# A two-block network on one core: in the feed-forward parts, gate and up are computed with tokens on partitions and turned, down moves both parts of its operand at once, and GpSimd's work there goes to ScalarE and VectorE

## The chip, the core and the metric

The kernel runs on one core of a Trainium2 chip. The metric is the device time of one execution in microseconds (us): the median of the kernel before is 1747.96 us over three runs (1747.33 to 1749.26). The engines are TensorE (PE; its weight loads are PEld), VectorE (DVE), ScalarE (ACT), GpSimd (POOL) and SyncE (SP), whose queue issues nearly all transfers.

## The reference

The input is 256 tokens of 1024 features in fp32. A first block of two layers is followed by a second block of one layer; the second block also reads 256 tokens of a context, and its modulation vectors come from two vectors `c` and `c_ctx`. Cut to what the change touches:

```
def swiglu_ffn(x, norm, w_gate, w_up, w_down):        # D_MODEL 1024, D_FF 2816
    h = rms_norm(x, norm)
    return (silu(h @ w_gate) * (h @ w_up)) @ w_down

for l in range(2):                                     # first block
    x = x + 0.5 * swiglu_ffn(x, ffn1_norm[l], ...)
    x = x + mixer(x)                                   # attention, chunk attention, retention
    x = x + 0.5 * swiglu_ffn(x, ffn2_norm[l], ...)

mx = silu(c) @ w_ada + b_ada                           # second block: six vectors of 1024
mc = silu(c_ctx) @ w_ada + b_ada                       # the same for the context (two are used)
x = x + gm_x * rms_norm(mixer2(modulate(rms_norm(x), ...), context))
x = x + gf_x * rms_norm(swiglu(modulate(rms_norm(x), ...), w_gate, w_up, w_down))
```

So there are five feed-forward parts: `ffn1` and `ffn2` in each of two layers, and one in the second block.

## The kernel before

Products keep nearly fp32 precision: every operand is split into a high part (`hi`, rounded to the short format fp32r) and a low part (`lo`, what is left), and `mm3` (L200) makes each product from three matmuls: low by high, high by low, high by high. Weights arrive in chunks of 1 MB (`load_now`, L170 to 192): SP issues the transfer into one of three `raw` buffers, ScalarE casts the high part (L189) and VectorE subtracts for the low part (L190), 1024 elements at a time, into four buffers each of `hi` and `lo`, which hold two chunks.

Activations lie with features on partitions: `x` is eight tiles of 128 features by 256 tokens, and `Stream` (L346) makes their two parts, `xh` and `xl`, as x comes.

`swiglu` (L363) runs gate and up in 22 steps of 128 hidden features. In a step the weights are the stationary operand and the tokens move: 2 x 8 x 3 = 48 matmuls of 256 columns. The two results share a PSUM bank. `gated` then multiplies them by 1/rms of each token (VectorE, L377), takes tanh (ScalarE), forms the product (VectorE L382, then GpSimd L384 in the first block, VectorE in the second), casts the high part `hh` (ScalarE, L386) and subtracts the low part `hl` (VectorE, L387). The result has hidden features on partitions, which is what the down product needs: 8 steps of 22 x 3 = 66 matmuls of 256 columns, with the weights stationary again. PSUM has a pool of four banks `mm` for these products and one of four banks `sm` for small ones.

Beside three of these parts (`ffn1` of layer 0, `ffn2` of layer 0, `ffn1` of layer 1) the modulation vectors are made (`ada`, L864): for each 128 features, 512 KB of weights `adaw` are multiplied by the silu of `c` and summed along the row. `swiglu` calls `tick` once a step, which asks for one more such piece. Where the piece is needed for two vectors, or is one of every second of the others, GpSimd multiplies and ScalarE sums (L886, L887); else VectorE does both in one instruction (L889). Beside `ffn2` of layer 1 the context is computed in the same way. The sums of squares for the norms are made by `Squares` (L222): seven squares and all additions on GpSimd, one square on ScalarE.

TensorE's order is that of the code. The order of the other engines is made by a scheduler that works with estimated times and priorities; loads are raised by 10 places (`AHEAD`).

Of the kernel before, what the change touches and what calls it, by code (L numbers as in the profile page):

```python
# [36 lines left out]
# columns of the per-feature table  # L37
# [12 lines left out]
# columns of a layer's row table, and of the second block's  # L50
# [10 lines left out]
def constants():  # L61
    """Tables that depend on shapes alone."""
# [42 lines left out]
def tile_kernel(ctx, tc, a):  # L105
# [35 lines left out]
    for half in range(2):  # L141
        xt = new(xp, [P, 4, T], "x", bufs=2)
        nc.sync.dma_start(xt.rearrange("p k t -> p (k t)"), a["xT"][half])
        x += [xt[:, k, :] for k in range(4)]
        if half == 0:
            first = new(wp, [P, RAW], "raw")
            for p in range(2):
                nc.sync.dma_start(first[:, half_sub(p)], a["wgu_ffn1"][0, 0, :, half_sub(p)])
    for p in range(2, 4):
        nc.sync.dma_start(first[:, half_sub(p)], a["wgu_ffn1"][0, 0, :, half_sub(p)])  # L150
# [14 lines left out]
    def load(src, n, eng=V):  # L165
        """A chunk of weights, and its two parts of 12 bits each."""
# [39 lines left out]
    def warm(n, bank=psm):  # L206
        """Products that nothing reads: they keep the tensor engine's clock up while it waits."""
# [6 lines left out]
    def rstd(ss, n, scale, eps, tag):  # L214
        """(ss * scale + eps) ** -0.5 over a few columns."""
# [6 lines left out]
    class Squares:  # L222
        """The sum of squares of each token, added up as the features come."""
# [4 lines left out]
        def add(self, t):  # L228
            self.n += 1
            if self.n == KD:  # L230
                q = new(tp, [P, T], "sqt", bufs=4)
                S.activation(q, t, AF.Square)
                if self.urgent:
                    self.parts = [self.acc, q]
                else:
                    G.tensor_tensor(self.acc, self.acc, q, op=ALU.add)
                    self.parts = [self.acc]
            elif self.acc is None:
                self.acc = new(tp, [P, T], "sqa", bufs=2)
                G.tensor_tensor(self.acc, t, t, op=ALU.mult)  # L240
            else:
                q = new(tp, [P, T], "sqt", bufs=4)
                G.tensor_tensor(q, t, t, op=ALU.mult)  # L243
                G.tensor_tensor(self.acc, self.acc, q, op=ALU.add)

        def by_token(self):
            """1/rms with tokens on partitions."""
# [15 lines left out]
        def along_row(self, keep=True):  # L263
            """The same along the free axis, on all partitions."""
# [11 lines left out]
    class QuickSquares(Squares):  # L276
        """The same of what comes in PSUM, with little left to do after the last part."""
# [29 lines left out]
    class DenseSquares(Squares):  # L307
        """The same, added up by the tensor engine, which it keeps busy between the parts."""
# [22 lines left out]
        def by_token(self):  # L331
            self.flush()
            # all rows are the same: the diagonal has each token on its partition
# [12 lines left out]
    class Stream:  # L346
        """What the next part of the first block needs of x, made as x comes."""
# [15 lines left out]
    def swiglu(xh, xl, sq, wgu, wd, fp, done, tick=lambda: None):  # L363
        """done(m, psum): each 128 output features of twice (four times with sq) the block's product."""
        hh, hl = [], []
        first_ks = [[k] for k in range(KD)] if sq is None else [range(KD - 2), range(KD - 2, KD)]
        # by then the sums of squares are there
        ready = 1 if first else 0

        def gated(gt, up, ps):  # L370
            if sq is not None:
                gu_t = new(fp, [P, 2, T], "gu", bufs=2)
                if ps is None:
                    for i, p in enumerate((gt, up)):
                        V.tensor_tensor(gu_t[:, i, :], p, sq.rb, op=ALU.mult)
                else:
                    V.tensor_tensor(gu_t, ps, bc_mid(sq.rb, 2), op=ALU.mult)  # L377
                gt, up = gu_t[:, 0, :], gu_t[:, 1, :]
            th = new(fp, [P, T], "th", bufs=2)
            S.activation(th, gt, AF.Tanh, scale=0.5)  # L380
            t1 = new(fp, [P, T], "t1", bufs=2)
            V.scalar_tensor_tensor(t1, th, 1.0, gt, op0=ALU.add, op1=ALU.mult)  # L382
            h = new(fp, [P, T], "h", bufs=2)
            (G if sq is not None else V).tensor_tensor(h, t1, up, op=ALU.mult)  # L384
            a_, b_ = new(fp, [P, T], "hh", F32R, bufs=KF), new(fp, [P, T], "hl", F32R, bufs=KF)
            S.copy(a_, h)  # L386
            V.tensor_tensor(b_, h, raw(a_), op=ALU.subtract)  # L387
            hh.append(a_)
            hl.append(b_)

        waiting = []
        for j in range(KF):
            w = load(wgu[j], 2 * D)
            if j or ready:
                ps = psm([P, 2, T])
                pss = [ps[:, gu, :] for gu in range(2)]
            else:
                # the last parts of x come late: the first product begins with the others
                ps = None
                pss = [psm([P, T]) for _ in range(2)]  # L400
# [1194 lines left out]
```

## Time and profile before

| | |
|---|---|
| device time, three runs | 1747.33, 1747.96, 1749.26 us |
| span of the profiled execution | 1745.7 us |
| median of the runs less this span | 2.3 us |
| TensorE matmul, busy | 1680.7 us (96%), 12837 instructions |
| TensorE weight load, busy | 1613.0 us (92%) |
| VectorE, busy | 1310.7 us (75%) |
| ScalarE, busy | 916.4 us (52%) |
| GpSimd, busy | 547.3 us (31%) |
| mean granted TensorE clock | 0.989 |
| transfers | 317.54 MB, mean 182 GB/s |

The profiled execution has no time of its own beside the span; the 2.3 us is what the median of the runs adds to it. A matmul's recorded duration is longer than the distance to the next one, since matmuls are pipelined; the cost of one in a row of many is the distance from start to start. In the profile's stretches, the number behind an engine's busy time is the count of its instructions there.

### The profile page before, as it was taken

The page shows a single profiled execution, that of the slowest core. Times are in us where ns is not written, and L with a number is a line of the kernel's source. Part 1 is how long each engine was busy: PE and PEld are TensorE (multiplying, and loading weights), DVE is VectorE, ACT ScalarE, POOL GpSimd, SP SyncE. Part 2 cuts the span into 40 slices and gives each one's busy share as a digit, 9 for nine tenths or more (in the row PEclk, how much of TensorE's full clock was granted, in tenths as well). Part 3 has the DMA queues.
Part 4 walks back from the last instruction along what each step waited for, and adds up shares of the span by engine and source line. Part 5 has one row for each costly group of instructions (what it writes and reads, how often), then busy time and mean ns, then how long its engine had stood idle before and what let it go on. Part 6 is the DMA issues. An engine that isn't in the chain of part 4 may idle for free. (4 is left out here: it accounts for less than half of the span.)

```text
span 1745.7 us, 31442 instructions
## 1 busy us (share of the span) xinstructions
PE 1680.7 (96%) x12837; PEld 1613.0 (92%) x12837; DVE 1310.7 (75%) x1755; ACT 916.4 (52%) x1491; POOL 547.3 (31%) x521
## 2 busy tenths in 40 slices
PE   8899999999999999999999999999999997999998
PEld 8789978899989999999987899999999996789997
DVE  8986678666899766986678766777887699766654
ACT  5554456634455544554456644455665564454443
POOL 5741242001466223651242101261333255410002
PEclk9999999999999999999999999999999998999999
DMA  8554664345477557764664435475445443035543
GB/s 315 196 197 155 207 225 166 124 145 190 170 260 267 183 167 266 282 242 162 193 246 145 167 124 172 156 259 196 165 144 171 142 150 129 26 132 182 186 155 119
DMA packets 55584, 317.54 MB, mean 182 GB/s; under 512 B 6160, under 2 KB 8592, under 8 KB 28816
## 3 DMA queue, kind: packets, MB, share of 16 engines
q1 hardware_dynamic: 51408, 307.45, 50.9%
q10 hardware_dynamic: 4032, 8.09, 1.3%
q8 instruction: 100, 1.64, 0.4%
q14 instruction: 44, 0.36, 0.1%
HBM read 314.46 MB, written 1.05 MB: 181 GB/s over the span
## 5 line engine op out<-in xcount | busy, mean ns | idle before, releaser
L190 DVE TENSOR_TENSOR lo<-raw,hi 128x1024 fp32r<-128x1024 f32 (+2 forms) x580 | 716.2, 1247 | 208.5 <-ACT hi L189 206.9
L189 ACT CAST hi<-raw 128x1024 fp32r<-128x1024 f32 (+2 forms) x584 | 562.9, 968 | 449.3 <-PE mm L204 360.9
L202 PE MATMUL mm<-xh,lo 128*128 128x256 f32 x2272 | 650.5, 286 | 29.8 <-DVE lo L190 29.8
L203 PE MATMUL mm<-xl,hi 128*128 128x256 f32 x2272 | 645.8, 284 | 0.1
L204 PE MATMUL mm<-xh,hi 128*128 128x256 f32 x2272 | 645.2, 284 | 0.0
L202 PEld LDWEIGHTS mm<-xh,lo 128*128 128x128 f32 x2272 | 438.4, 193 | 36.2 <-DVE lo L190 34.8
L203 PEld LDWEIGHTS mm<-xl,hi 128*128 128x128 f32 x2272 | 438.4, 193 | 0.6 <-DVE xl L953 0.3
L204 PEld LDWEIGHTS mm<-xh,hi 128*128 128x128 f32 x2272 | 438.4, 193 | 0.0
L202 PE MATMUL mm<-hh,lo 128*128 128x256 f32 x880 | 246.9, 281 | 0.0
L203 PE MATMUL mm<-hl,hi 128*128 128x256 f32 x880 | 246.6, 280 | 0.0
L204 PE MATMUL mm<-hh,hi 128*128 128x256 f32 x880 | 246.6, 280 | 0.0
L384 POOL TENSOR_TENSOR h<-t,gu 128x256 f32<-128x256 f32 x88 | 105.1, 1196 | 248.3 <-DVE t L382 248.3
L203 PEld LDWEIGHTS mm<-hl,hi 128*128 128x128 f32 x880 | 165.6, 188 | 0.0
L202 PEld LDWEIGHTS mm<-hh,lo 128*128 128x128 f32 x880 | 165.6, 188 | 0.0
L204 PEld LDWEIGHTS mm<-hh,hi 128*128 128x128 f32 x880 | 165.6, 188 | 0.0
L202 PE MATMUL mm<-hi,xl 128*128 128x512 f32 (+2 forms) x320 | 127.6, 399 | 5.6 <-ACT uT L1274 5.6
L204 PE MATMUL mm<-hi,xh 128*128 128x512 f32 (+2 forms) x320 | 124.5, 389 | 0.0
L203 PE MATMUL mm<-lo,xh 128*128 128x512 f32 (+2 forms) x320 | 124.5, 389 | 0.0
L243 POOL TENSOR_TENSOR sqt<-x 128x256 f32<-128x256 f32 x42 | 55.7, 1327 | 144.3 <-DVE x L433 138.9
L203 PE MATMUL mm<-yl,hi 128*128 128x256 f32 x336 | 94.8, 282 | 2.5 <-DVE yl L846 2.5
L202 PE MATMUL mm<-yh,lo 128*128 128x256 f32 x336 | 95.0, 283 | 0.0
L204 PE MATMUL mm<-yh,hi 128*128 128x256 f32 x336 | 94.6, 281 | 0.0
(321 smaller groups left out, 2363.5 us busy)
## 6 DMA issues: line engine op xcount, KB each, us to landing
raw<-in_wgu_ffn SPq DMA_DIRECT2D x86, 1024.0 KB, 4.8
raw<-in_wd_ffn SPq DMA_DIRECT2D x64, 704.0 KB, 4.0
raw<-in_w_in_b SPq DMA_DIRECT2D x36, 1024.0 KB, 5.0
adaw<-in_w_ada SPq DMA_DIRECT2D x48, 512.0 KB, 5.3
raw<-in_w_gates SPq DMA_DIRECT2D x24, 1024.0 KB, 4.7
raw<-in_wgu SPq DMA_DIRECT2D x22, 1024.0 KB, 4.7
raw<-in_w_in SPq DMA_DIRECT2D x13, 1024.0 KB, 4.8
raw<-in_w_branch SPq DMA_DIRECT2D x12, 1024.0 KB, 4.8
```

What stands on the lines that cost most here:

```text
L189: S.copy(hi[:, c:e], r[:, s + c:s + e])
L190: eng.tensor_tensor(lo[:, c:e], r[:, s + c:s + e], raw(hi)[:, c:e], op=ALU.subtract)
L202: PE.matmul(out, sl, mh, start=start, stop=False)
L203: PE.matmul(out, sh, ml, start=False, stop=False)
L204: PE.matmul(out, sh, mh, start=False, stop=stop)
L243: G.tensor_tensor(q, t, t, op=ALU.mult)
L384: (G if sq is not None else V).tensor_tensor(h, t1, up, op=ALU.mult)
```

## The change

- **Gate and up.** The stationary operand is now 128 tokens of x, and the weights move: 11 steps of 256 hidden features, each with two chunks of 1 MB and two banks (one for each half of the tokens, gate in columns 0 to 255 and up in 256 to 511): 8 x 2 x 3 = 48 matmuls of 512 columns. The weights are laid out for that.
- **gated.** Tokens lie on partitions, so 1/rms is a scalar for each partition and goes into tanh's scale and into one of two VectorE instructions for each half of the tokens; `along_row`, which made a row of 1/rms by two small matmuls, falls away here. `tick` is called after each half, 22 times.
- **turned.** Four transposes (fp32, 128 x 128) on TensorE turn the product of a step into a PSUM bank of the pool `sm`; ScalarE casts the high part and VectorE subtracts the low part, 512 elements each. TensorE does this after the first half of the second next step, and for the last step after the first half of the first down step.
- **Down.** In the first block's four parts, `mm3_split` moves the high and the low part side by side against the high weights, one matmul of 512 columns, and the high part against the low weights, one of 256; `done` adds the two halves of the bank to x with two instructions instead of one. The second block's part keeps three matmuls of 256.
- **Modulation vectors.** All of them are on VectorE (L911), one instruction for each vector and piece, with a `tick` for each.
- **Squares.** All squares on ScalarE, all additions on VectorE.
- The context's sequence waits 11 ticks instead of 9 at one place, and takes 29 instead of 27. Comments are removed.

```
     class Squares:
         def add(self, t):
             self.n += 1
-            if self.n == KD:
-                q = new(tp, [P, T], "sqt", bufs=4)
-                S.activation(q, t, AF.Square)
...
-            elif self.acc is None:
+            if self.acc is None:
                 self.acc = new(tp, [P, T], "sqa", bufs=2)
-                G.tensor_tensor(self.acc, t, t, op=ALU.mult)
...
+                S.activation(self.acc, t, AF.Square)
+                return
+            q = new(tp, [P, T], "sqt", bufs=4)
+            S.activation(q, t, AF.Square)
+            if self.n == KD and self.urgent:
+                self.parts = [self.acc, q]
             else:
...
+                V.tensor_tensor(self.acc, self.acc, q, op=ALU.add)
+                self.parts = [self.acc]

+    def mm3_split(out, st, mv, start, stop):
+        sh, sl = st
+        if not start:
+            PE.matmul(out[:, 0], sl, mv[:, 0], start=False, stop=False)
+        PE.matmul(out, sh, mv, start=start, stop=stop)
+        if start:
+            PE.matmul(out[:, 0], sl, mv[:, 0], start=False, stop=False)

+        def gated(pss):
+            hs = []
+            for t in range(NT):
+                g, u = pss[t][:, 0:T], pss[t][:, T:2 * T]
+                th = new(fp, [P, T], "th", bufs=2)
+                S.activation(th, g, AF.Tanh, scale=scale["hr"][:, t:t + 1] if sq is not None else 0.5)
+                V.scalar_tensor_tensor(th, th, 1.0, g, op0=ALU.add, op1=ALU.mult)
+                h = new(fp, [P, T], "h", bufs=4)
+                if sq is not None:
+                    V.scalar_tensor_tensor(h, th, scale["r2"][:, t:t + 1], u, op0=ALU.mult, op1=ALU.mult)
+                else:
+                    V.tensor_tensor(h, th, u, op=ALU.mult)
+                hs.append(h)
+                tick()
+            return hs
+
+        def turned(hs):
+            ps = psq([P, 2, T])
+            for t in range(NT):
+                for i in range(2):
+                    transpose_to(ps[:, i, t * P:(t + 1) * P], hs[t][:, i * P:(i + 1) * P])
+            o = new(fp, [P, 2, 2, T], "hx", F32R, bufs=KF // 2)
+            S.copy(o[:, 0], ps)
+            V.tensor_tensor(o[:, 1], ps, raw(o)[:, 0], op=ALU.subtract)
+            hx.append(o)
+        for j in range(n2):
+            pss = [psm([P, 512]) for _ in range(NT)]
+            for half in range(2):
+                w = load(wgu[j, :, half * 4:(half + 1) * 4, :].rearrange("p k c -> p (k c)"), 2048)
+                for kk in range(4):
+                    k = half * 4 + kk
+                    for t in range(NT):
+                        s = slice(t * P, (t + 1) * P)
+                        mm3(pss[t], (xh[k][:, s], xl[k][:, s]), part(w, kk * 512, 512), k == 0, k == KD - 1)
...
+                if half == 0 and made and j > 2:
+                    turned(made.pop(0))
...
+                    mv = hx[k // 2][:, :, k % 2, :]
+                    if split:
+                        mm3_split(ps, part(w, kk * P, P), mv, k == 0, k == KF - 1)
...
+                if made:
+                    turned(made.pop(0))
             done(m, ps)
...
         def done(m, ps):
-            V.scalar_tensor_tensor(x[m], ps, 0.25, x[m], op0=ALU.mult, op1=ALU.add)
+            for half in range(2):
+                V.scalar_tensor_tensor(x[m], ps[:, half], 0.25, x[m], op0=ALU.mult, op1=ALU.add)
...
                 for i in reversed(range(n)):
-                    if i or (n == 1 and m % 2):
-                        t = new(pool, [P, D], "adaj") if i else r
-                        G.tensor_tensor(t, r, rows[:, i, :], op=ALU.mult)
-                        S.activation(t, t, AF.Copy, scale=0.5, accum_out=total)
...
+                    V.scalar_tensor_tensor(
+                        new(pool, [P, D], "adaj") if i else r, r, 0.5, rows[:, i, :], op0=ALU.mult, op1=ALU.mult,
+                        accum_out=mod[:, i * 48 + m:i * 48 + m + 1],
+                    )
+                    yield
```

What the change does to the order is shown at two places. The first is TensorE in gate and up of the first feed-forward part; `xh`, `xl` are the parts of x, `hi`, `lo` those of the weights, `mm` a bank of results. Before:

```order
L202 MATMUL mm_242<-xh_113,lo_235 128x256
L203 MATMUL mm_242<-xl_114,hi_234 128x256
L204 MATMUL mm_242<-xh_113,hi_234 128x256
L202 MATMUL mm_242<-xh_119,lo_235 128x256
L203 MATMUL mm_242<-xl_120,hi_234 128x256
```

Now, at the end of the third step (`sm` is the bank into which `h`, the product of the first step, is turned):

```order
L203 MATMUL mm_358<-lo_400,xh_161 128x512
L204 MATMUL mm_358<-hi_399,xh_161 128x512
L455 MATMUL sm_427<-ident_77,h_327 128x128 x2
L455 MATMUL sm_427<-ident_77,h_332 128x128 x2
L202 MATMUL mm_450<-hi_454,xl_114 128x512
L203 MATMUL mm_450<-lo_455,xh_113 128x512
```

The matmuls have 512 columns instead of 256, half as many to a product, and once in a step four transposes stand among them.

The second place is VectorE in the same part: `lo` is the low part of weights, and the instructions that write `adaw` or `adaj` make the modulation vectors. Before, from one chunk of weights to the next (`gu`, `t`, `hl` belong to `gated`):

```order
L190 TENSOR_TENSOR lo_634<-raw_631,hi_633 128x1024
L382 SCALAR_TENSOR_TENSOR t_72_390<-th_388,gu_386 128x256
L889 SCALAR_TENSOR_TENSOR adaw_702,mod_95<-adaw_702,silu_469 128x1024
L382 SCALAR_TENSOR_TENSOR t_84_461<-th_459,gu_457 128x256
L190 TENSOR_TENSOR lo_638<-raw_631,hi_637 128x1024
L377 TENSOR_TENSOR gu_530<-mm_481,trb_360 128x512
L190 TENSOR_TENSOR lo_711<-raw_708,hi_710 128x1024
```

Now, over a chunk and a half (`th` belongs to `gated`, `hx` is the turned product):

```order
L190 TENSOR_TENSOR lo_459<-raw_452,hi_458 128x1024
L911 SCALAR_TENSOR_TENSOR adaj_816,mod_95<-adaw_814,silu_334 128x1024
L190 TENSOR_TENSOR lo_497<-raw_494,hi_496 128x1024
L911 SCALAR_TENSOR_TENSOR adaw_814,mod_95<-adaw_814,silu_334 128x1024
L911 SCALAR_TENSOR_TENSOR adaj_909,mod_95<-adaw_907,silu_334 128x1024
L391 SCALAR_TENSOR_TENSOR th_435<-th_435,mm_357 128x256
L391 SCALAR_TENSOR_TENSOR th_444<-th_444,mm_358 128x256
L190 TENSOR_TENSOR lo_501<-raw_494,hi_500 128x1024
L408 TENSOR_TENSOR hx_432<-sm_427,hx_432 128x512
L911 SCALAR_TENSOR_TENSOR adaw_907,mod_95<-adaw_907,silu_334 128x1024
L911 SCALAR_TENSOR_TENSOR adaj_1002,mod_95<-adaw_1000,silu_334 128x1024
```

More vector instructions now stand between two chunks' low parts, and they stand early: all 24 of this part come before the weights of the eighth of 11 steps.

## Rows read from the trace of the kernel before

**Rows 1.** The page's busy time, share of the span and instructions of each engine.
```profile
span 1745.7 us, 31442 instructions
...
PE 1680.7 (96%) x12837; PEld 1613.0 (92%) x12837; DVE 1310.7 (75%) x1755; ACT 916.4 (52%) x1491; POOL 547.3 (31%) x521
```
**Rows 2.** The page's groups: busy, mean ns; idle time before, what ended it.
```profile
L202 PE MATMUL mm<-xh,lo 128*128 128x256 f32 x2272 | 650.5, 286 | 29.8 <-DVE lo L190 29.8
```
**Rows 3.** Stretches: busy us (instructions) of PE, PEld, DVE, ACT, POOL; clock, DMA, GB/s.
```profile
40.00:120.00 80.00, 67.44 (x544) 65.41 (x543) 77.86 (x85) 42.96 (x69) 50.77 (x30) 1.00 0.57 198
500.00:560.00 60.00, 53.20 (x424) 52.12 (x423) 59.91 (x69) 32.06 (x53) 40.35 (x22) 0.97 0.70 246
700.00:780.00 80.00, 74.30 (x598) 73.27 (x598) 76.56 (x83) 42.30 (x68) 49.70 (x28) 0.98 0.73 264
...
560.00:640.00 80.00, 80.00 (x671) 80.00 (x670) 54.15 (x74) 40.01 (x60) 17.93 (x17) 1.00 0.54 180
1560.00:1640.00 80.00, 80.00 (x669) 80.00 (x668) 50.77 (x70) 38.75 (x56) 0.00 (x0) 1.00 0.52 185
...
20.00:40.00 20.00, 20.00 (x170) 20.00 (x169) 18.02 (x18) 10.97 (x16) 9.37 (x5) 1.00 0.85 326
```
**Rows 4.** Timeline of PE, gate and up (start us, us, instruction); 44 matmuls start to start.
```profile
149.73 0.28 PE L202 MATMUL mm<-xh,lo 128*128 128x256 f32 x1
...
155.01 0.28 PE L204 MATMUL mm<-xh,hi 128*128 128x256 f32 x1
```
**Rows 5.** Timeline of PE in a mixer, 512 columns, 42 starts after the first; then small matmuls.
```profile
224.84 0.39 PE L204 MATMUL mm<-hi,xh 128*128 128x512 f32 x1
...
234.39 0.39 PE L204 MATMUL mm<-hi,xh 128*128 128x512 f32 x1
234.62 0.61 PE L267 MATMUL sm<-ident,trr 128*128 128x128 f32 x4
234.98 0.48 PE L202 MATMUL mm<-hi,xl 128*128 128x512 f32 x1
```
**Rows 6.** Timeline of PE, down product with four transposes in it; 18 starts follow 1340.75.
```profile
1340.07 0.28 PE L204 MATMUL mm<-hh,hi 128*128 128x256 f32 x1
1340.20 0.60 PE L428 MATMUL sm<-ident,cxo 128*128 128x128 f32 x4
1340.55 0.36 PE L202 MATMUL mm<-hh,lo 128*128 128x256 f32 x1
1340.75 0.28 PE L203 MATMUL mm<-hl,hi 128*128 128x256 f32 x1
...
1342.88 0.28 PE L203 MATMUL mm<-hl,hi 128*128 128x256 f32 x1
```
**Rows 7.** The transposes of one line: duration ns min/median/max, first and last start.
```profile
L428 PE MATMUL sm<-ident,wide x120: 270/272/330, 284.6 to 1063.1; 128*128 128x128 f32 x120
```
**Rows 8.** The chain that ended last: six matmuls with a moving operand in four pieces.
```profile
1511.67 1.39 PE sm L212 x6
```
**Rows 9.** Timeline of DVE beside the modulation vectors (start us, us).
```profile
63.89 0.68 DVE L377 TENSOR_TENSOR gu<-mm,trb 128x512 f32<-128x512 f32 x1
64.50 1.21 DVE L190 TENSOR_TENSOR lo<-raw,hi 128x1024 fp32r<-128x1024 f32 x1
65.63 0.41 DVE L387 TENSOR_TENSOR hl<-h,hh 128x256 fp32r<-128x256 f32 x1
65.96 1.22 DVE L889 SCALAR_TENSOR_TENSOR adaw<-adaw,silu 128x1024 f32<-128x1024 f32 x1
67.11 0.08 DVE L889 DVE_READ_ACCUMULATOR adaw<-adaw,silu 128x1 f32 x1
67.11 3.40 DVE L190 TENSOR_TENSOR lo<-raw,hi 128x1024 fp32r<-128x1024 f32 x1
70.43 0.41 DVE L382 SCALAR_TENSOR_TENSOR t<-th,gu 128x256 f32<-128x256 f32 x1
```
**Rows 10.** Timeline of POOL in the same stretch.
```profile
66.14 3.28 POOL L886 TENSOR_TENSOR adaj<-adaw,silu 128x1024 f32<-128x1024 f32 x1 [1.59 <-ACT adaj L887]
```
**Rows 11.** The low parts in 1560 to 1640 us: duration ns min/median/max.
```profile
L190 DVE TENSOR_TENSOR lo<-raw,hi x28: 1224/1225/1227, 1561.3 to 1638.8; 128x1024 fp32r<-128x1024 f32 x28
```

More of the change, by code (lines that the diff above doesn't have):

```diff
@@ L361, in add @@
             self.sq.add(x[k])
[L363 to L375, printed above, removed]
-                else:
[L377 to L400, printed above, removed]
-            for ks in [range(KD)] if j or ready else first_ks:
-                for gu in range(2):
-                    for k in ks:
-                        mm3(pss[gu], part(w, gu * D + k * P, P), (xh[k], xl[k]), k == 0, k == KD - 1)
-            waiting.append((*pss, ps))
-            if sq is not None and j <= ready:
-                if j == ready:
-                    sq.by_token()
-                continue
-            if sq is not None and j == ready + 1:
-                sq.along_row()
-            for each in waiting:
-                gated(*each)
-            waiting = []
-            tick()
@@ new lines, in mm3_split, with swiglu, tokens_ready @@
+    def mm3_split(out, st, mv, start, stop):
[5 more added lines that the diff above has]
+            PE.matmul(out[:, 0], sl, mv[:, 0], start=False, stop=False)
+    def swiglu(xh, xl, sq, wgu, wd, fp, done, tick=lambda: None, split=False):
+        by_first = bool(first)
+        scale = {}
+        hx = []
+        def tokens_ready():
+            sq.by_token()
+            hr = new(tp, [P, NT], "hrs")
+            V.tensor_scalar(hr, sq.r, 0.5, None, op0=ALU.mult)
+            r2 = new(tp, [P, NT], "r2s")
+            V.tensor_tensor(r2, sq.r, sq.r, op=ALU.mult)
+            scale.update(hr=hr, r2=r2)
+        def gated(pss):
[8 more added lines that the diff above has]
+                    V.scalar_tensor_tensor(h, th, scale["r2"][:, t:t + 1], u, op0=ALU.mult, op1=ALU.mult)
+                else:
+                    V.tensor_tensor(h, th, u, op=ALU.mult)
[11 more added lines that the diff above has]
+            hx.append(o)
+        made, waiting = [], []
+        n2 = KF // 2
+        for j in range(n2):
[7 more added lines that the diff above has]
+                        mm3(pss[t], (xh[k][:, s], xl[k][:, s]), part(w, kk * 512, 512), k == 0, k == KD - 1)
+                if sq is not None and j == 1 and half == 0 and by_first:
+                    tokens_ready()
+                if half == 0 and made and j > 2:
+                    turned(made.pop(0))
+            if sq is not None and j == 0 and not by_first:
+                tokens_ready()
+            waiting.append(pss)
+            if j == 0 and sq is not None:
+                continue
+            if j == 2 and made:
+                turned(made.pop(0))
+            while waiting:
+                made.append(gated(waiting.pop(0)))
+        while len(made) > 1:
+            turned(made.pop(0))
@@ L439, in ffn @@
                 cur.hi, cur.lo, cur.sq, a[f"wgu_{which}"][l], a[f"wd_{which}"][l], fp, done,
-                lambda: next(other, None),
+                lambda: next(other, None), split=True,
             )
@@ L1060, in context @@
             sq.add(t)
-        for _ in range(9):
+        for _ in range(11):
             yield
@@ L1501, in tile_kernel @@
         fill = context(h0, cx)
-        ffn(LAYERS - 1, "ffn2", lambda pool: (next(fill) for _ in range(27)), cur, nxt)
+        ffn(LAYERS - 1, "ffn2", lambda pool: (next(fill) for _ in range(29)), cur, nxt)
         next(fill)
```

28 lines of the change are left out of this document (8 added, 20 removed).

## The prediction

> **What bounds the kernel now.** I read the page's busy times first: TensorE is busy for 1680.7 of 1745.7 us, every other engine for at most 75% [rows 1]. So its instructions and its gaps set the time. The groups say who ends the gaps: the first matmul of a chunk of weights waits 29.8 us in all for the low part that VectorE makes, and hardly for anything else [rows 2]. The stretches say where. Two undisturbed stretches of 80 us hold 671 and 669 matmuls; beside the modulation vectors 40 to 120 us holds 544, 500 to 560 us holds 424 of some 502, and 700 to 780 us holds 598 [rows 3]. At 0.120 us each that is 15.1 + 9.4 + 8.5 = 33.0 us lost, a granted clock of 0.97 and 0.98 included. VectorE is busy there for 77.86, 59.91 and 76.56 us, that is nearly all the time, and GpSimd for well over half [rows 3].
>
> The timelines say why VectorE is late. A low part of 1024 elements follows the one before it by 1.13 us when free (64.50 to 65.63); the one that starts while GpSimd multiplies a modulation vector from 66.14 to 69.42 takes 3.40 us instead of 1.21 [rows 9, 10]. From 1560 us on, with GpSimd idle, all 28 take 1.22 to 1.23 us [rows 3, 11]. So a large instruction of GpSimd holds up VectorE, VectorE holds up TensorE, and the rest of the kernel is TensorE's own rate.
>
> **The change part by part.** *Gate and up.* Per feed-forward part before: 22 x 48 = 1056 matmuls of 256 columns at 5.28/44 = 0.120 us [rows 4], 126.7 us. Now: 11 x 48 = 528 of 512 columns. A mixer has this very form, weights moving against tokens: 9.55/42 = 0.2274 us [rows 5], 120.1 us. That is 6.6 us less, 33.2 us in five parts. All of it lies on the path.
>
> *Down.* In the first block, three matmuls of 256 columns at 2.13/18 = 0.1183 us [rows 6] become one of 512 and one of 256: 0.3550 to 0.3457 us, 0.0093 us for each of 4 x 8 x 22 = 704 products, 6.5 us less. The moving operand lies in two pieces; six matmuls of 512 columns in four pieces took 1.39 us, 0.23 each [rows 8], so I charge pieces nothing. If they cost so much that one of 512 takes as long as two of 256, the gain is 0.
>
> *Transposes.* From 1340.07 to 1340.75 there are two matmul steps and four transposes: 0.68 - 0.24 = 0.44 us for four [rows 6]. 55 groups (11 in each of five parts) add 24.2 us. TensorE waits for `h` at each. It was asked for a step and a half before (some 16 us), in the last step half a down step before (3.8 us) against tanh, two VectorE instructions for each half and the queue between, about 3 us; I charge nothing, and 1 us for each of five parts if that cover is gone.
>
> The Trainium skill, "TensorE: Matmul & The Clock Gate", Part 4 (PE-mode transpose), speaks against this part: it gives about 275 ns for a transpose in a kernel, bound by access latency, which would be 220 x 0.275 = 60.5 us. The trace has that number as a duration, 272 ns [rows 7], but not as a distance; by the rule the forecast would be 1742, by the rows 1706.
>
> *Small terms.* `along_row` falls away in four parts, 2 x 0.09 us each [rows 5]: 0.7 us less. The second instruction in `done` lies on the path where the next part waits for x, 0.4 us as row 70.43 has it [rows 9], once: after `ffn2` of layer 1. At the other ends the next product begins with other features, and this covers it. Squares add some 0.4 us for each tile to ScalarE and VectorE; in the down steps VectorE has about 5 of 7.6 us to do, so they cost nothing there; at the start they stand before the first cast, 0 to 2 us, of which I take 0 since GpSimd no longer slows the first low parts. TensorE's sum: -33.2 - 6.5 + 24.2 - 0.7 + 0.4 = -15.8 us.
>
> *The stalls.* With GpSimd out, each VectorE instruction keeps its free price, start to start: 1.14 us for 1024 elements, 0.61 for 512 (63.89 to 64.50), about 0.36 for 256 (65.63 to 65.96 is 0.33) [rows 9]. But VectorE has 64 vectors to make instead of 32, the scheduler puts them early, and a low part queues behind them. So I count, in the changed order, VectorE's work from one chunk's low parts to the next, against 24 x 0.2274 + 0.22 = 5.68 us that TensorE takes for a chunk. `ffn1` of layer 0, from the fifth chunk: 5.9, 12.1 (two low parts, six vectors, eight instructions of 256), 4.6, 8.9, 5.2, 5.4, 5.9, 5.3, 4.8, then at most 3.7. VectorE falls 8.7 us behind. `ffn2` of layer 0: 5.7, 7.1, 5.3, 11.7, 5.7, 6.8, 5.2: 8.1 us behind. `ffn1` of layer 1: never over 6.2, 1 us behind. What can be borne: a low part may be made when TensorE has done half of the second-last chunk, 1.5 chunks ahead, 8.5 us, less its cast and itself, about 2: 6.5 us. So TensorE waits some 2 us in each of the first two parts and 0 in the third. Transfers: in `ffn2` of layer 0 SP now issues 16 vectors' pieces among six chunks, 14.7 MB; at the 326 GB/s that one stretch reaches [rows 3] this is 45 us against 34 us of TensorE, and the lead of up to four chunks covers most of the 11 us. I take 4 us for transfers in all. Of the 33.0 us, 8 stay and 25 go. The bounds: all 33.0 go, or none.
>
> Behind the waiting low parts stand the casts' buffers, and so SP's next transfer; nothing else waits for them.
>
> *Sum.* 1745.7 - 15.8 - 25 = 1704.9 us of span. The runs' median lies 2.3 us above the span, as before: 1707. I round to 1706, since the clock's loss in the stalled stretches goes as well where no gap is left.
>
> **The rivals.** *The stalls stay.* VectorE takes the place of GpSimd: 41 us of vectors instead of half of that, placed early, and a transfer that is late blocks the low part behind it. For it: the 12.1 and 11.7 us above, and VectorE's 77.86 of 80 us now [rows 3]. Against it: in that stretch much of VectorE's time is waiting for GpSimd, as the 3.40 us show [rows 9], and the third part has no such heap. Then the 25 us don't come: 1731.
>
> *Transposes cost their duration.* Each holds TensorE for its 272 ns [rows 7]: 59.8 us instead of 24.2, 1742. Against it stands 0.44 us for four [rows 6]; for it only that this is one place, among matmuls of 256 columns.
>
> *Slower: the banks.* A step now fills two of the four `mm` banks, so step j+2 can't start until VectorE has read both banks of step j, four instructions behind whatever stands in its queue; before, a step filled one, and one instruction of 512 elements freed it. If every one of the 55 steps waits for one instruction of 1024 elements, 1.22 us [rows 11], that is 67 us: 1773. It makes the kernel slower from 42/55 = 0.76 us in a step on. For it: `gated` is not raised in the order as loads are. Against it: a whole step, 10.9 us, lies between, and VectorE without GpSimd is busy for 50.77 of 80 us [rows 3].
>
> **How the numbers follow.** The forecast, 1706 us, gets 0.70; its own range is 1697 (no stall stays) to 1720 (14 us more stay). The stalls stay, 1731: 0.15. Transposes by duration, 1742: 0.05. The banks, 1773: 0.06. The other 0.04 is for gains and losses that cancel within 0.2%, some 3.5 us, which is about what a measurement of this kernel can tell from no change. The first three are all faster by more than that: 0.90; the same 0.04; slower 0.06. The range must take in nearly all of the first case and most of the second: 1693 (all stalls gone and 4 us of the start and the clock with them) to 1732.
>
> **What would show it.** In the changed profile: about 0.227 us from start to start in gate and up and 0.346 us for a product in down; 220 more transposes that cost 0.11 us each; GpSimd nearly idle in the feed-forward parts, and low parts at 1.2 us throughout; the idle time of TensorE before its first matmul of a chunk down from 29.8 us to about 10, what is left of it in the first 80 us and after 480 us. If low parts are short and TensorE still waits for them in those places, the heap of vectors is the cause; if it waits with VectorE idle on a vector's data, the transfers; if it waits at a step's first matmul for `gated`, the banks. The forecast is wrong if the time is above 1720 or below 1697.

## The result and the profile after

The changed kernel takes 1719.03 us (median of four runs, 1718.54 to 1720.25), the kernel before 1748.35 us (four runs, 1747.33 to 1749.26): a ratio of 0.9831, 95% interval 0.9817 to 0.9845. It is 29.3 us faster, where 42 were forecast; the time is 13 us above the forecast and inside its range.

The page's busy times and the group of the first matmul of three, which answer to [rows 1, 2]:

```profile
span 1716.8 us, 24933 instructions
...
PE 1665.1 (97%) x9697; PEld 1459.4 (85%) x9697; DVE 1245.0 (73%) x1872; ACT 896.5 (52%) x1424; POOL 213.0 (12%) x274
...
L202 PE MATMUL mm<-hi,xl 128*128 128x512 f32 (+1 forms) x1200 | 477.6, 398 | 16.9 <-DVE h L394 8.9
```

GpSimd fell from 547.3 to 213.0 us. TensorE's wait before a chunk is no longer for the low part: what ends most of it now is `h`, the last instruction of `gated`, 8.9 of 16.9 us. The stretches, as in [rows 3] (busy time and instructions of PE, PEld, DVE, ACT and POOL; clock, DMA share, GB/s):

```profile
20.00:40.00 20.00, 16.34 (x68) 12.72 (x68) 17.43 (x30) 7.89 (x10) 0.71 (x1) 0.93 0.90 342
40.00:60.00 20.00, 20.00 (x92) 16.48 (x91) 20.00 (x34) 9.05 (x11) 0.00 (x0) 0.98 0.80 273
480.00:500.00 20.00, 14.74 (x62) 11.85 (x61) 18.76 (x34) 6.86 (x9) 1.62 (x1) 0.87 0.90 305
500.00:520.00 20.00, 20.00 (x91) 16.46 (x89) 19.54 (x35) 8.61 (x11) 0.00 (x0) 0.96 0.94 338
700.00:780.00 80.00, 80.00 (x368) 66.23 (x367) 63.43 (x94) 38.73 (x49) 0.00 (x0) 1.00 0.68 250
1560.00:1640.00 80.00, 80.00 (x368) 66.29 (x367) 49.32 (x64) 36.94 (x49) 0.00 (x0) 1.00 0.51 173
```

The third part with modulation vectors (700 to 780 us) now holds as many matmuls as the undisturbed last one, 368. The first two still lose time, once each, near 35 and near 495 us.

The stages, from their first matmul to the next stage's first; the forecast column is put together from the prediction's terms (in gate and up 10 of the 11 groups of transposes, the last one in down):

| stage | before, us | after, us | change | forecast |
|---|---|---|---|---|
| gate/up, `ffn1` of layer 0 | 145.4 | 132.7 | -12.8 | -15.5 |
| gate/up, `ffn2` of layer 0 | 137.0 | 132.4 | -4.7 | -5.8 |
| gate/up, `ffn1` of layer 1 | 136.1 | 124.8 | -11.3 | -10.9 |
| gate/up, last part | 127.3 | 124.4 | -2.9 | -2.2 |
| down, these three of the first block | 62.7 each | 62.5 each | -0.2 each | -1.2 each |
| down, last part (to its last matmul) | 59.8 | 62.6 | +2.8 | +0.4 |
| `ffn2` of layer 1, with the context | 236.9 | 235.7 | -1.2 | -3.2 |
| start, mixers, tail | 715.3 | 716.8 | +1.5 | 0 |

Where nothing disturbs it, gate and up came as forecast. Down gained next to nothing, and in the last part, where its code still makes three matmuls of 256 columns, it became slower. TensorE's timeline shows both (start us, us, instruction). First the changed kernel's gate and up with a group of transposes in it, and an undisturbed stretch:

```profile
703.20 0.39 PE L204 MATMUL mm<-hi,xh 128*128 128x512 f32 x1
703.44 0.60 PE L455 MATMUL sm<-ident,h 128*128 128x128 f32 x4
703.79 0.48 PE L202 MATMUL mm<-hi,xl 128*128 128x512 f32 x1
704.10 0.40 PE L203 MATMUL mm<-lo,xh 128*128 128x512 f32 x1
...
706.42 0.39 PE L204 MATMUL mm<-hi,xh 128*128 128x512 f32 x1
...
709.82 0.39 PE L204 MATMUL mm<-hi,xh 128*128 128x512 f32 x1
```

From 706.42 to 709.82 are 15 starts, 0.227 us each, as in [rows 5]. From 703.20 to 704.10 are two steps, 0.455 us, and four transposes, 0.445 us, as in [rows 6]. Then the split down product in the first block (nine products, one matmul of 256 and one of 512 columns each, from 146.19 to 149.38):

```profile
146.19 0.28 PE L363 MATMUL mm<-hx,lo 128*128 128x256 f32 x1
146.31 0.40 PE L364 MATMUL mm<-hx,hi 128*128 128x512 f32 x1
...
149.38 0.28 PE L363 MATMUL mm<-hx,lo 128*128 128x256 f32 x1
```

That is 0.354 us for a product (0.353 over the stage), not 0.346: 0.117 for 256 columns and 0.235 to 0.236 for 512. And the last part, first before, then after; between the two rows shown lie 24 starts each time:

```profile
1699.77 0.28 PE L202 MATMUL mm<-hh,lo 128*128 128x256 f32 x1
...
1702.49 0.28 PE L202 MATMUL mm<-hh,lo 128*128 128x256 f32 x1
```

```profile
1669.85 0.28 PE L202 MATMUL mm<-hx,lo 128*128 128x256 f32 x1
...
1672.67 0.28 PE L202 MATMUL mm<-hx,lo 128*128 128x256 f32 x1
```

0.1133 us before and 0.118 after, for the same three matmuls of 256 columns by the same code (`mm3`), at a granted clock of 1.00 in both.

What was left of the stalls is in the main one wait in each of the first two parts. VectorE's timeline in the changed kernel before the first one, and TensorE's at the second:

```profile
31.01 1.22 DVE L911 SCALAR_TENSOR_TENSOR adaj<-adaw,silu 128x1024 f32<-128x1024 f32 x1
...
32.16 1.22 DVE L190 TENSOR_TENSOR lo<-raw,hi 128x1024 fp32r<-128x1024 f32 x1
33.30 0.41 DVE L391 SCALAR_TENSOR_TENSOR th<-th,mm 128x256 f32<-128x256 f32 x1
33.63 1.22 DVE L911 SCALAR_TENSOR_TENSOR adaw<-adaw,silu 128x1024 f32<-128x1024 f32 x1
...
34.77 0.41 DVE L391 SCALAR_TENSOR_TENSOR th<-th,mm 128x256 f32<-128x256 f32 x1
35.10 1.22 DVE L911 SCALAR_TENSOR_TENSOR adaj<-adaw,silu 128x1024 f32<-128x1024 f32 x1
...
36.25 0.47 DVE L394 SCALAR_TENSOR_TENSOR h<-th,r2s,mm 128x256 f32<-128x256 f32 x1
```

```profile
491.58 0.39 PE L204 MATMUL mm<-hi,xh 128*128 128x512 f32 x1
497.23 0.77 PE L202 MATMUL mm<-hi,xl 128*128 128x512 f32 x1 [5.26 <-DVE h L394]
497.79 0.63 PE L203 MATMUL mm<-lo,xh 128*128 128x512 f32 x1
...
501.21 0.50 PE L202 MATMUL mm<-hi,xl 128*128 128x512 f32 x1
501.55 0.40 PE L203 MATMUL mm<-lo,xh 128*128 128x512 f32 x1
501.78 0.40 PE L204 MATMUL mm<-hi,xh 128*128 128x512 f32 x1
```

In the code `gated` of step 0 stands behind step 1, within which 1/rms is made; by then the two steps hold two of the four `mm` banks each. On VectorE the instructions that read the banks (L391, L394) stand among modulation vectors (L911). Low parts are short now, 1.22 us, but TensorE stands for 5.26 us until a bank is free. Behind the wait its granted clock is 0.87 over 480 to 500 us: eight starts from 497.79 to 501.21 are 0.4275 us apart (1.2 GHz), then 0.23 again (2.4 GHz).

### The profile page after: what moved, and what is told of

Read it like the earlier page. It is cut to its first block, busy times and chain, and to the rows that moved or that the text cites. A ratio compares the mean times of both kernels' runs of the same rounds, so it can differ in the third digit from the quotient of the medians.

```text
span 1716.8 us, 24933 instructions
## 1 busy us (share of the span) xinstructions
PE 1665.1 (97%) x9697; PEld 1459.4 (85%) x9697; DVE 1245.0 (73%) x1872; ACT 896.5 (52%) x1424; POOL 213.0 (12%) x274
## 5 line engine op out<-in xcount | busy, mean ns | idle before, releaser
L202 PE MATMUL mm<-hi,xl 128*128 128x512 f32 (+1 forms) x1200 | 477.6, 398 | 16.9 <-DVE h L394 8.9
L204 PE MATMUL mm<-hi,xh 128*128 128x512 f32 (+1 forms) x1200 | 469.4, 391 | 0.0
L203 PE MATMUL mm<-lo,xh 128*128 128x512 f32 (+1 forms) x1200 | 468.9, 391 | 0.2 <-DVE lo L190 0.2
L364 PE MATMUL mm<-hx,hi 128*128 128x512 f32 x704 | 247.6, 397 | 1.3 <-DVE hx L408 1.3
L202 PE MATMUL mm<-xh,lo 128*128 128x256 f32 x512 | 146.2, 286 | 0.2 <-DVE lo L190 0.2
L204 PE MATMUL mm<-xh,hi 128*128 128x256 f32 x512 | 144.8, 283 | 0.0
L203 PE MATMUL mm<-xl,hi 128*128 128x256 f32 x512 | 144.8, 283 | 0.0
L363 PEld LDWEIGHTS mm<-hx,lo 128*128 128x128 f32 x672 | 126.7, 189 | 1.3
L202 PEld LDWEIGHTS mm<-xh,lo 128*128 128x128 f32 x512 | 98.2, 192 | 1.2 <-DVE wide L758 0.7
L203 PEld LDWEIGHTS mm<-xl,hi 128*128 128x128 f32 x512 | 98.2, 192 | 0.0
L204 PEld LDWEIGHTS mm<-xh,hi 128*128 128x128 f32 x512 | 98.2, 192 | 0.0
```

The source lines that it names most:

```text
L202: PE.matmul(out, sl, mh, start=start, stop=False)
L203: PE.matmul(out, sh, ml, start=False, stop=False)
L204: PE.matmul(out, sh, mh, start=False, stop=stop)
L363: PE.matmul(out[:, 0], sl, mv[:, 0], start=False, stop=False)
L364: PE.matmul(out, sh, mv, start=start, stop=stop)
```

## The experiments

Each ratio is against the kernel before, timed beside it. The experiments are told in the order of the questions: the stalls, the price of the transposes, then down.

**The old form without GpSimd.** One part of the change alone, in the kernel before:

```diff
-            (G if sq is not None else V).tensor_tensor(h, t1, up, op=ALU.mult)
+            V.tensor_tensor(h, t1, up, op=ALU.mult)
...
-                    if i or (n == 1 and m % 2):
-                        t = new(pool, [P, D], "adaj") if i else r
-                        G.tensor_tensor(t, r, rows[:, i, :], op=ALU.mult)
-                        S.activation(t, t, AF.Copy, scale=0.5, accum_out=total)
...
+                    V.scalar_tensor_tensor(
+                        new(pool, [P, D], "adaj") if i else r, r, 0.5, rows[:, i, :], op0=ALU.mult, op1=ALU.mult,
+                        accum_out=mod[:, i * 48 + m:i * 48 + m + 1],
+                    )
+                    yield
...
-                G.tensor_tensor(mod[:, s], mod[:, s], pv[:, b0 + c * 4:b0 + c * 4 + 4], op=ALU.add)
+                V.tensor_tensor(mod[:, s], mod[:, s], pv[:, b0 + c * 4:b0 + c * 4 + 4], op=ALU.add)
```

> The kernel before with one part of the change alone: modulation vectors and the product h on VectorE, none of them on GpSimd, one vector at each tick; gate and up, down and squares as before. Theory 'GpSimd holds VectorE': low parts fall from 1.33 to 1.26 us in the mean, and of the 36.9 us that gate and up of the first three parts lost, some 20 go, as in the changed kernel: 1728 us. Rival 'VectorE is full': its own work grows by 38 vectors of 1.14 and 88 products of 0.33 us, 72 us, nothing is gained: 1748 us or more.

1727.67 us, ratio 0.9894 (0.9879 to 0.9909), 18.9 us less than before in the same comparison. The waits of TensorE in this kernel (us in total, times, longest):

```profile
PE mm L202 <- DVE gu L377: 10.3, 5, 6.4
...
PE mm L202 <- DVE lo L190: 3.8, 3, 2.9
```

The wait for low parts went from 29.8 to 3.8 us, though VectorE has more to do; gate and up of the first three parts went from 145.4, 137.0 and 136.1 us to 140.9, 128.5 and 129.0, 20 us less. So GpSimd's hold on VectorE was the cause, as [rows 9, 10] said, and two thirds of the whole gain need nothing else of the change. The Trainium skill, "SBUF — State Buffer", "Who interferes with whom", has the rule: an instruction of VectorE with two inputs in SBUF contends with one of GpSimd that reads SBUF, and the later one waits. The trace agrees, 3.40 us against 1.21. The old form, too, is left with a wait for its banks, at the instruction that empties them (L377).

**Short vectors.** In the changed kernel the modulation vectors are summed over 16 of 1024 features.

```diff
-                        new(pool, [P, D], "adaj") if i else r, r, 0.5, rows[:, i, :], op0=ALU.mult, op1=ALU.mult,
+                        (new(pool, [P, D], "adaj") if i else r)[:, :16], r[:, :16], 0.5, rows[:, i, :16], op0=ALU.mult, op1=ALU.mult,
```

> The modulation vectors are summed over 16 of their 1024 features: all transfers stay, VectorE's instruction falls from 1.14 to about 0.1 us. Theory 'queue': every stall beside them goes, 8.2 + 8.0 + 0.4 us in gate and up of the first three parts, 1703 us. Rival 'transfers': the stalls of ffn2 in layer 0 stay, where 365 GB/s were moved, and 1711 to 1719 us come out.

1703.21 us, ratio 0.9747 (0.9733 to 0.9760). Gate and up of the three parts: 127.1, 124.8, 124.8 us. No wait for a bank is left, though the transfers of this stretch run at 397 GB/s, against 314 in the changed kernel:

```profile
475.00:500.00 25.00, 25.00 (x113) 20.66 (x113) 18.11 (x52) 12.37 (x16) 0.66 (x1) 1.00 1.00 397
```

So the stalls left by the change were VectorE's queue, not the transfers. The 2.7 us that the first part still takes over the last part's 124.4 lie at its very beginning: from 10.67 to 13.23 us its starts are 0.427 us apart (1.2 GHz), and the granted clock is 0.77 over 8.5 to 12 us. The kernels before and after begin in the same way, so in their first parts too this much isn't a stall of the vectors.

**One buffer.** One instead of three for the incoming matrix, which spreads the vectors in VectorE's order.

```diff
-            t = new(pool, [P, D], "adaw", bufs=3)
+            t = new(pool, [P, D], "adaw", bufs=1)
...
-                r = new(pool, [P, D], "adaw", bufs=3)
+                r = new(pool, [P, D], "adaw", bufs=1)
```

> One buffer instead of three for the incoming modulation matrix: in the changed order VectorE then has two modulation vectors in a step of gate and up, after the step's four reading instructions, instead of up to six early. Theory 'queue' (TensorE's waits for its banks, 3.7 and 5.3 us, come since gated stands behind the vectors in VectorE's queue, and the clock falls behind each wait): gate and up of ffn1 and of ffn2 in layer 0 fall from 132.6 and 132.4 us to about 125, 1719 - 15 = 1704 us. Rival 'transfers' (the stalls come from the transfers of the modulation matrix, which compete with the weights and stand before them in SP's queue): the stalls stay or grow, since each transfer now waits for VectorE while it stands before a chunk's: 1719 to 1730 us.

1711.99 us, ratio 0.9797 (0.9781 to 0.9812). Half right. The waits of 3.7 and 5.3 us for `h` shrank to 0.6 and 0, and the first two parts fell to 128.2 and 127.5 us. But `ffn1` of layer 1 rose from 124.8 to 131.4 us, with a new wait:

```profile
PE mm L203 <- DVE lo L190: 4.1, 5, 1.6
```

**Spread.** One buffer where a transfer serves two vectors, three where it serves one.

```diff
+        nb = 1 if n == 2 else 3
...
-                r = new(pool, [P, D], "adaw", bufs=3)
+                r = new(pool, [P, D], "adaw", bufs=nb)
```

> One buffer for the modulation matrix in the two parts where each transfer serves two vectors, three again in ffn1 of layer 1, where it serves one. Theory 'queue': gate and up of the first three parts about 128.2 and 127.5 (as with one buffer throughout, 1712 us) and 124.8 us (as in the changed kernel, against 131.4 with one buffer): 1712 - 6.6 = 1705.5 us. If the third part's 131.4 had another cause than its single buffer, 1712.

1708.26 us, ratio 0.9780 (0.9767 to 0.9794): 128.2, 125.6 and 124.8 us. The single buffer was the third part's trouble. Of the some 17 us that the changed kernel loses in these parts (132.7, 132.4 and 124.8 against the last part's 124.4), 11 are gone, and half of the rest is the first part's beginning.

**Turned twice.**

```diff
-                    transpose_to(ps[:, i, t * P:(t + 1) * P], hs[t][:, i * P:(i + 1) * P])
+                    for _ in range(2):
+                        transpose_to(ps[:, i, t * P:(t + 1) * P], hs[t][:, i * P:(i + 1) * P])
```

> Each transpose of h is made twice into the same bank, 220 more. By the prediction's step 0.44 us for four: 55 x 0.44 = 24.2 us more than the changed kernel, 1743 us. By the rival that each costs its duration, 220 x 0.272 = 59.8 us more, 1779. If half of a transpose lies in time that TensorE waits anyway, 1731.

1740.26 us, ratio 0.9960 (0.9948 to 0.9973), 21.2 us above the changed kernel: 0.39 us for four transposes in the mean of 55 groups, 0.10 each. In the last part's gate and up, ten groups more took 4.4 us (128.8 against 124.4), 0.44 each. The count by starts was right, the one by durations wrong.

**Side by side.** The first guess at down was the prediction's own proviso, the two pieces of the moving operand.

```diff
-            S.copy(o[:, 0], ps)
-            V.tensor_tensor(o[:, 1], ps, raw(o)[:, 0], op=ALU.subtract)
+            S.copy(o[:, :, 0], ps)
+            V.tensor_tensor(o[:, :, 1], ps, raw(o)[:, :, 0], op=ALU.subtract)
...
-                    mv = hx[k // 2][:, :, k % 2, :]
+                    mv = hx[k // 2][:, k % 2]
```

> The two parts of a down product lie side by side, so that the 512-column matmul moves one piece of 512 and not two of 256 at a distance. Changed kernel: 0.235 us for that matmul and 0.117 for the one of 256 beside it, 62.6 us for a down stage of the first block. Theory 'pieces' (a matmul in two pieces of 256 takes as long as two of 256): the 512-column one falls to gate and up's 0.227, 704 x 0.008 = 5.6 us in four parts, 1713.4 us, each down stage 61.2 us. Rival 'pair' (the 0.235 belongs to a 512-column matmul that stands between two of 256 under new weights, whatever it moves): 0.235 stays, 1719 us. The last part's down stage is the same in both, 62.6 us.

1718.21 us, ratio 0.9831 (0.9817 to 0.9844), no change; down of `ffn1` in layer 0 takes 62.28 us from its first to its last matmul, as in the changed kernel. Two pieces cost no more than one here; that theory fell. What the 512 columns cost more than in gate and up (0.235 against 0.227) stays without a cause.

**Three of 256.**

```diff
-                        mm3_split(ps, part(w, kk * P, P), mv, k == 0, k == KF - 1)
+                        mm3(ps, part(w, kk * P, P), mv, k == 0, k == KF - 1)
...
+            if sq is None:
+                o = [new(fp, [P, 2, T], nm, F32R, bufs=KF // 2) for nm in ("hh", "hl")]
```

> The down product is three matmuls of 256 columns in all five parts, with one instruction in done; in the last part alone the two parts of the product lie in two tiles of their own, as in the kernel before. The prediction's step (0.3457 us for a split product, 0.3550 for three): 704 x 0.0093 = 6.5 us slower, less 0.4: 1725. Theory 'pieces' (the split product took 0.353, three of 256 at 0.118 take 0.354): 704 x 0.001 = 0.7 us, 1719.5 in the four parts. Last part: if it's the tile that both parts share that made its down matmul 0.118 instead of 0.113 us, its down stage falls from 62.6 to 60 us and the sum to 1717; if not, it stays at 62.6.

1724.74 us, ratio 0.9868 (0.9855 to 0.9881): 5.7 us above the changed kernel. The split does save about what the prediction's step said, 6.5 less 0.4: each of the three down stages that stand alone takes 63.9 us instead of 62.5. But the three matmuls that it replaces cost more in this kernel than before; between the rows shown lie 24 starts, in this kernel and in the kernel before:

```profile
619.87 0.28 PE L202 MATMUL mm<-hx,lo 128*128 128x256 f32 x1
...
622.75 0.28 PE L202 MATMUL mm<-hx,lo 128*128 128x256 f32 x1
```

```profile
639.91 0.28 PE L202 MATMUL mm<-hh,lo 128*128 128x256 f32 x1
...
642.76 0.28 PE L202 MATMUL mm<-hh,lo 128*128 128x256 f32 x1
```

0.1200 against 0.1188 us. The separate tiles of the last part changed nothing (0.118). So the same matmul of 256 columns has at least four prices in these kernels, each the same through an undisturbed stage. What goes with them is the place of the moving tile: the distance of its start from that of the weights in SBUF, modulo 256 bytes, by the allocation of the built kernels (in these stages `hi` and `lo` always lie at 96). It is -64 for `hh` in the last part before (0.1133), +64 for `hx` there after (0.118), +128 for `hh` in the first parts before (0.1188), 0 for `hx` in the first parts here (0.1200).

**Shifted tiles.** On top of 'spread', unused bytes ahead of tiles.

```diff
+GAPS = {(0, 'ffn1'): 128, (0, 'ffn2'): 96, (1, 'ffn1'): 224, (1, 'ffn2'): 0}
...
+    gap = ctx.enter_context(tc.tile_pool(name="gap", bufs=1))
     xp = ctx.enter_context(tc.tile_pool(name="xp", bufs=8))
...
+    new(gap, [P, 16], "gap")
...
+            if GAPS[l, which]:
+                new(fp, [P, GAPS[l, which] // 4], "gap")
...
+        new(fq, [P, 16], "gap")
```

> As 'spread', and unused bytes set ahead of some tiles: 64 before the tiles of x, and 96 to 288 ahead of those of the feed-forward parts, so that the parts of h (hx) begin at other places against the weights (hi, lo), counted modulo 256 bytes: in the five parts -64, -96, +32, -96 (as it comes out for the fourth: 256) and -64; the weights against x, which move in gate and up: from 0 to -64. Why: between runs the same matmul of 256 columns starts every 0.113, 0.118, 0.119 or 0.120 us, constant within a stage, and these go with the place of the moving tile: 0.120 at a distance of 0 (x in all kernels, hx of 'three of 256', yh after the change), 0.119 at +128 (hh and yh before), 0.118 at +64 and -32, 0.113 at -64 (hh in the last part before). Theory 'distance to the weights': gate and up's 512 columns fall from 0.227 to about 0.220 us, 2640 x 0.007 = 18.5 us and some 6 in the mixers; down of the first part from 0.353 to about 0.340 us a product, of the last from 0.118 to 0.113: 4.9 us; 256 columns of x in the mixers at +64 0.118: 2 us. Against 'spread' (1705 to 1712) 31 us less, 1675 to 1681. Theory 'own place' (the moving tile's own place modulo 256 counts): gate and up stay at 0.227, the down stages gain as above: 7 us less, 1698 to 1705. Rival 'no place' (what set the rates goes with something else): no change against 'spread'.

1715.06 us, ratio 0.9820 (0.9806 to 0.9833): slower than 'spread' by 6.8 us, which neither theory said, but place it is. The last part's down fell to 0.1133 us at -64 (24 starts between the first two rows shown), 62.6 to 60.4 us with its transposes. Gate and up rose, at a place of the weights against x of -64 instead of 0 (21 starts between the other two):

```profile
1669.87 0.28 PE L207 MATMUL mm<-hx,hi 128*128 128x256 f32 x1
...
1672.59 0.28 PE L207 MATMUL mm<-hx,hi 128*128 128x256 f32 x1
```

```profile
699.86 0.39 PE L207 MATMUL mm<-hi,xh 128*128 128x512 f32 x1
...
704.76 0.39 PE L207 MATMUL mm<-hi,xh 128*128 128x512 f32 x1
```

4.90/21 = 0.2333 us against 0.2267. The tiles that move there lie where they lay; those held still were shifted. So the moving tile's own place alone doesn't set the price. The distance of the two fits both cases, but no run shifts both tiles together and keeps their distance, so that it is the distance, and not the place of whichever tile was shifted, is not shown. What is best for 256 columns is worse for 512.

The split product, expected at 0.340 us, gained nothing at -64. Seven products there, and seven in `ffn2` of layer 0, where `hx` lies at -96:

```profile
144.98 0.28 PE L366 MATMUL mm<-hx,lo 128*128 128x256 f32 x1
...
147.45 0.28 PE L366 MATMUL mm<-hx,lo 128*128 128x256 f32 x1
```

```profile
601.52 0.28 PE L366 MATMUL mm<-hx,lo 128*128 128x256 f32 x1
...
603.95 0.28 PE L366 MATMUL mm<-hx,lo 128*128 128x256 f32 x1
```

That is 0.353 us, as at 0, and 0.347; at +32, in `ffn1` of layer 1, it is 0.347 too.

**The kernel before, shifted.** The cleanest test: only unused bytes are added.

```diff
+GAPS = {(0, 'ffn1'): 64, (0, 'ffn2'): 64, (1, 'ffn1'): 64, (1, 'ffn2'): 224}
...
+            if GAPS[l, which]:
+                new(fp, [P, GAPS[l, which] // 4], "gap")
```

> The kernel before, and nothing but unused bytes ahead of the tiles of four feed-forward parts (64, 64, 64 and 224), so that hh and hl lie at -64 bytes modulo 256 against the weights, as they did in the last part alone. Theory 'place': the down matmul of 256 columns falls in these parts from 0.1187 (0.1183 in layer 1's ffn2) to the last part's 0.1134 us, each down stage from 62.5 to 59.8 us, four of them: 11 us less, 1737. Rival 'last part' (it's something else in the last part that makes its matmuls 0.113): no change, 1747.

1738.06 us, ratio 0.9944 (0.9931 to 0.9956): 10.2 us less for nothing but the place of the tiles in four pools; of these, TensorE's matmuls of 256 columns move `hh` and `hl`. 24 starts, in `ffn2` of layer 0:

```profile
629.75 0.28 PE L204 MATMUL mm<-hl,hi 128*128 128x256 f32 x1
...
632.47 0.28 PE L204 MATMUL mm<-hl,hi 128*128 128x256 f32 x1
```

0.1133 us, 59.75 us for a down stage instead of 62.54, in three of the four shifted parts; the fourth, beside the context, has 0.113 us by its starts too.

**Three at 32, and x too.** Both on top of 'spread', with three matmuls of 256 columns and gaps that put `hx` at -64 (it starts at 32, the weights at 96); the second shifts x by 192 bytes as well. The edit of the first, and what the second has in place of its gaps:

```diff
+GAPS = {(0, 'ffn1'): 192, (0, 'ffn2'): 192, (1, 'ffn1'): 192, (1, 'ffn2'): 96}
...
-                lambda: next(other, None), split=True,
+                lambda: next(other, None), split=False,
...
+        new(fq, [P, 32], "gap")
```

```diff
+GAPS = {(0, 'ffn1'): 0, (0, 'ffn2'): 0, (1, 'ffn1'): 0, (1, 'ffn2'): 160}
...
+    new(gap, [P, 48], "gap")
...
+        new(fq, [P, 48], "gap")
```

> 'Spread', and in all five parts three matmuls of 256 columns for a down product, with hx at -64 bytes modulo 256 against the weights; x where it was. Theory 'place': three at 0.1134 take 0.340 us instead of 0.353: each down stage 59.9 us with its one group of transposes, instead of 62.5: five times 2.6 us below 'spread', and 0.4 us for the one instruction in done: 1695 us. If the price of three stays at 0.118 to 0.120: 1708 to 1714.

1697.96 us, ratio 0.9721 (0.9707 to 0.9734), 3 us above what was expected; each of the four down stages that stand alone takes 60.3 us from its first to its last matmul. Three well placed (0.340 us) beat the split at every place where it ran alone (0.347 to 0.353).

> As 'three at 32', and 192 bytes ahead of the tiles of x, so that x lies at -64 against the weights, where 256 columns of it move (1250 matmuls of the mixers and of layer 1's ffn2 and after), and the weights at +64 against x where they move by 512. The first gain, by the price of 256 columns at -64: 1250 x 0.0066 = 8 us. The second has no run yet: 512 columns took 0.2274 at 0 and 0.2335 at -64; +64 may give either or less. With 0.227: 1687 us; with 0.2335: 3600 x 0.006 = 22 us more, 1709.

1692.90 us, ratio 0.9679 (0.9666 to 0.9692): the fastest, 26 us below the changed kernel. 256 columns of x now take 0.114 to 0.115 us. 512 columns at +64 take 0.229 (six starts here), a little more than the 0.227 at 0, which in 2640 matmuls of gate and up is most of the 6 us above the 1687 expected:

```profile
704.58 0.39 PE L207 MATMUL mm<-hi,xh 128*128 128x512 f32 x1
...
705.95 0.39 PE L207 MATMUL mm<-hi,xh 128*128 128x512 f32 x1
```

## Why the prediction was right, and where it was not

*Gate and up, transposes: right.* 0.227 us and 0.445 us for four stand in the trace. The undisturbed last part takes 124.4 us, where the prediction's terms make 120.1 + 4.4; it fell by 2.9 us and not by 2.2 since the kernel before took 127.3 us there and not 126.7. All 55 groups of transposes cost 21 us by 'turned twice', instead of 24.2. The rival of their duration is out.

*Stalls: the mechanism of before right, what is late next wrong.* Against the last part's 127.3 us, gate and up of the first three parts lost some 37 us before; after, against 124.4, they lose some 17. So 20 went, not 25, and twice the forecast's 8 stayed. The step counted VectorE's backlog against the time at which a low part is needed. But low parts are raised in the order and `gated` is not; the backlog fell on `gated`, and so on the banks. That is the rival 'the banks', with its mechanism and its sign of a step's first matmul waiting for `gated`, only not in 55 steps but in one step of each of two parts, where two steps' results lie unread; the prediction's "a whole step lies between" doesn't hold there. The transfers, for which 4 us were set aside, cost nothing that 'short vectors' shows. That the 4 us covered a part of the banks' price was luck.

*Down: the step that failed.* The step priced 256 columns at 0.1183 us and 512 at 0.2274 wherever they move. The split itself gave 5.7 us against three at the same place ('three of 256'), where 6.1 were forecast, but by other prices: 512 columns took 0.235 us there, and two of 256 took 0.240. The change put `hx` where a product of three costs 0.360 us (63.74 us a stage, first to last matmul) instead of 0.356 (62.54), so that the split came out at 0.353, and in the last part, where nothing was split, 0.1133 became 0.118: 2.4 of the 2.8 us there, the rest is its transposes. In these stages and `ffn2` of layer 1 this is about 7.5 us, the largest part of the 12 us by which the span of 1716.8 misses 1704.9; the stalls are some 5, gate and up gave 2 back, and mixers and start took 1.5. Of that, 1.2 has the same cause: in the mixers 960 matmuls that move `yh` and `yl` went from 0.1187 us at +128 to 0.1200 at 0. [Rows 8] didn't carry the step either: 1.39/6 is 0.232, not 0.227, and I rounded both to 0.23 in a term worth 0.009 a product. Nor does its operand lie in four pieces: `warm` reads one piece of 128 columns of ones four times. The last part's 0.1133 stood in the trace of before, and the prediction didn't use it.

*Small terms.* GpSimd is nearly idle in these parts, and low parts take 1.22 us there, as said. The forecast came out near enough since its errors, nearly all to one side, were small beside gate and up, and GpSimd's hold.

## What to carry to other kernels

Price a matmul by starts from the stage where it will run, and compare the same form in different stages first: where the prices differ at one clock, shift a tile before rewriting its loop. When a stall's cause is taken away, ask which reader is next in that engine's queue, above all one that frees PSUM banks and has no priority. In this kernel VectorE's queue could be spread by the number of buffers that feed it: one was better where a transfer serves two vectors, three where it serves one.

## What was not expected of the hardware

The interval between matmuls goes with how far apart the moving and the held operand start in SBUF, modulo 256 bytes: 256 columns in three 0.1133 us at -64, 0.118 at +64, 0.1188 at +128, 0.1200 at 0; 512 columns in gate and up 0.227 at 0, 0.229 at +64, 0.233 at -64, at a granted clock of 1.00. That the place of the tiles causes it is shown by the gaps. The distance alone is not the whole of it: in the split product, at 0 as well, 256 columns took 0.117 and 512 took 0.235. Why, and why 256 and 512 want different distances, was not explained, and other distances were not tried for 512 columns in gate and up.

The Trainium skill, "SBUF — State Buffer", "Who interferes with whom", gives TensorE one port for the moving operand and one for weight loads, independent of each other. Taken by itself, that gives no reason why the gaps in 'the kernel before, shifted' should change anything; they gave 10.2 us, and the measurement decides.
